# Four reorderings and one unsplit weight matrix in a two-layer decoder trunk

## The chip, the core and the metric

The kernel runs on one core of one Trainium2 chip. The metric is the device time of one launch in microseconds (us). The time before is 1378.09 us, the median of 3 runs (1377.64 to 1379.01).

## What is computed

The reference takes `x` (1 x 256 x 1024, float32) through two layers. Cut to what matters here, a layer is:

```python
u = x @ w_in[i]                                  # 1024 -> 512 pool + 512 value + 512 gate
y_pool = pool_mixer(u_pool, pool_w[i], pool_scale[i])
v = u_val * sigmoid(u_gate)                      # causal depthwise convolution, 31 taps, on v
y_conv = silu(layer_norm(conv(v) + b_dw)) @ conv_pw[i]
x = layer_norm(ALPHA * x + concat(y_pool, y_conv) @ w_out[i])
f = swiglu(x, w1, w3, w2)              if i == 0          # dense, 2816 wide
f = sum over the top 2 of 8 experts of gate * swiglu(x)   # i == 1, 3584 wide each
x = layer_norm(ALPHA * x + f)
x = x + sigmoid(x @ ple_gate_w[i]) * (p[i] @ ple_w[i])    # the embedding's gate
```

All weights are float32; those of the eight experts alone are 352 MB.

## The kernel before

**Tiles.** The 256 tokens are two halves `h` of 128 rows. Activations lie row by row in `xr[h]` (128 x 1024) and, for the matmuls, transposed in `xT[h]`. A float32 product is made as three matmuls of a cheaper type, float32r: each operand is split into a rounded part H and a rest L, and H·H, H·L and L·H are summed (`mm`, L339 to L349). `to_xT` (L335) transposes four 128 x 128 blocks on TensorE (L332), rounds them on ScalarE (L317) and takes the rest on VectorE (L318).

**Weights.** The class `Weights` (L75) holds one list of all weight items in the order of their use. `advance` (L122) loads each piece of 1 MB through SyncE's queue (L114), rounds it on ScalarE (L143, the "cast") and takes the rest on VectorE (L158, "the rests"). Loads, rounded items and temporaries share a pool of 19 slots; `hl` limits the slots of live rounded items, `temps` is set aside for temporaries, and `cap` says up to which item a `get` may go ahead of what it needs. `prepare(name, n)` makes items now, `n` of them or all. Names in `DIRECT` (L38) are not split: they are used as loaded, with the unrounded activations `x.f`, in one float32 matmul each (L341).

**Order.** Every engine runs its instructions in the order in which the program names them; nothing is scheduled behind its back. So where a `prepare` stands decides what its casts and rests delay. Six places matter here.

1. The start. L298 and L299 make the matrix `shift` (used first by the narrow experts' `fold`, L1044) from `con`, a block of constants; L299 is ScalarE's first instruction. Then come warm-up matmuls, `table(AF.Sigmoid)`, and at L1197 to L1199 the splits of the two halves of `x` and the first weights (`wg00`, `wv00`).
2. `mixer` (L462) begins with `diagonals(0)` (L494, L497): 16 ScalarE instructions that make the diagonal matrices of eight convolution taps; `conv(0)` (L503) uses them. In the second layer `value(0, 0, late)` carries in its middle the transposes of the second half of `xr` (`late`), and `gate(0, 1)` is the first that needs them.
3. `moe` (L838): the first expert's first matrix `w1e0_0` is multiplied with both halves, and between the matmuls of the second half the router's (L859, L861) and the sort of its results (`route`, L940; `positions`, L973) are placed:

```python
        W.prepare("w3e0_0", None)
        table(AF.Sigmoid)
        ...
        proj(ids, p1[0], xT[0])
        to_xT(xT[1], xr[1], 0)
        router(0, range(KD))
        to_xT(xT[1], xr[1], 1)
```

4. `experts` (L1037): 55 blocks of one expert's 512 hidden columns each, with first matrix `w1`, third `w3`, and the block before's `w2`. In the last block `cap` stands below the second item of the previous `w2` until that is needed (L1062, L1094).
5. The end of `moe`, L919 to L938: `last(h)` adds the last expert to `yacc[h]`, the norm of each half follows (`norm_begin`, then `norm_apply` for two column blocks, L413 and L414), `emit` makes the embedding, and `prepare` makes the gate's weights between them.
6. `embed_gate` (L1138) for the last layer: for column block c = 0 both halves, then for c = 1 both halves, the very last in two pieces of 256 columns (L1157). The second half's transposes are `late(0)` and `late(1)`, in the first of the four products.

Of the kernel before, what the change touches and what calls it, by code (L numbers as in the profile page):

```python
# [17 lines left out]
P = 128  # L18
# [3 lines left out]
KD = D // P  # L22
# [12 lines left out]
ND = len(DENSE_CHUNKS)  # L35
SLOTS = 19
HL_START, HL_PRE, HL_FIRST, HL_SECOND, HL_MOE = 8, 12, 8, 6, 10
DIRECT = ("pw0", "pw1", "wo00", "wo01")  # L38
DT = 23
MORE_AT = 53  # L40
WARM = 16
# [4 lines left out]
WU_EARLY = 2  # L46
# [5 lines left out]
EM = 3, 0  # L52
GL = 6
END = ((0, 256), (256, 256))
# [139 lines left out]
def trunk(ctx: ExitStack, tc: tile.TileContext, a: dict, out: bass.AP):  # L194
    nc = tc.nc
# [9 lines left out]
    def acc(name, k=None):  # L205

        if k is None:
            k = at[0] % 4
            at[0] += 1
        return pacc.tile([P, 512], F32, tag=f"acc{k}", name=name)  # L210
# [85 lines left out]
    H = P // 2  # L296
    shift = cp.tile([P, P], F32R, name="shift")
    nc.gpsimd.memset(shift[:, H:].bitcast(F32), 0.0)  # L298
    nc.scalar.copy(shift[:, :H], ident[:, H:])  # L299
    wr = tl("m2", [KD, NE])  # L300
    nc.gpsimd.dma_start(wr, a["router"])
    neghalf = cp.tile([P, 1], F32, name="neghalf")
# [19 lines left out]
    def new_xT(f=None):  # L322
        return [Split(tl(f"xH{h}", [KD, P], F32R), tl(f"xL{h}", [KD, P], F32R), None if f is None else f[:, h])
                for h in range(2)]
# [10 lines left out]
    def to_xT(dst, src, c):  # L335

        split_into(dst[:, 4 * c:4 * c + 4, :], transposes(src[:, c * 512:(c + 1) * 512], 4))
# [124 lines left out]
    def mixer(l, xT, xr, late, loads):  # L462
# [31 lines left out]
        def diagonals(b):  # L494
            for i in range(2):
                for k in range(TAPS - DT):
                    nc.scalar.activation(dg[:, i * 8 + k], ident, AF.Copy, scale=weight(2 * b + i, DT + k))  # L497
# [8 lines left out]
        def gate(b, h, between=None):  # L506
            pg = acc("ps_g")
            proj(W.names[f"wg{b}{l}"], pg, xT[h], free=h == 1, also=lambda k: k == GB and between and between())
            nc.scalar.activation(vb[b][h], pg[:, :256], AF.Sigmoid)

        def value(b, h, between=None):
            pv = acc("ps_v")
            proj(W.names[f"wv{b}{l}"], pv, xT[h], free=h == 1, also=lambda k: k == GB and between and between())
            nc.vector.tensor_mul(vb[b][h], pv[:, :256], vb[b][h])
# [3 lines left out]
            copy(vT[b][:, :, 32 + h * P:32 + (h + 1) * P], transposes(vb[b][h], 2))  # L518

        W.temps = TEMPS_MIX  # L520
        diagonals(0)

        gate(0, 0)
        if l == 0:
            gate(0, 1)
            value(0, 0)
        else:
            value(0, 0, late)
            gate(0, 1)
        W.prepare(f"wg1{l}")  # L530
        value(0, 1, lambda: turn(0, 0))
# [306 lines left out]
    def moe(l, xr, gb1, mix, project):  # L838
# [6 lines left out]
        sc = norm_begin(xr[1], mix[1], lambda: to_xT(xT[0], xr[0], 1))  # L845
        for c in range(2):
            norm_apply(gb1, xr[1], sc, c)
        W.prepare("w3e0_0", None)
        table(AF.Sigmoid)

        p1 = [acc("p1") for _ in range(2)]
# [13 lines left out]
        to_xT(xT[1], xr[1], 0)  # L865
        router(0, range(KD))
        to_xT(xT[1], xr[1], 1)
        W.hl = HL_SECOND
        routed = []

# [45 lines left out]
        last = experts(ranks, gates, xr, yacc, (selT, gsl, xg), lambda: hidden(g, 512, 0),  # L916
                       lambda: over(ci, beyond, gate, xr, yacc), end)
        gb, (ple, emit, _) = late["gains"], late["ple"]
        xT2 = new_xT()  # L919
        table(AF.Sigmoid)  # L920
        last(0)
        sc = [norm_begin(yacc[0], None)]
        W.prepare(f"gate0{l}", 2)
        emit(EM[0])
        for c in range(2):
            norm_apply(gb, yacc[0], sc[0], c)
        to_xT(xT2[0], yacc[0], 0)
        emit(EM[1])
        last(1)
        W.prepare(f"gate0{l}", 3)  # L930
        to_xT(xT2[0], yacc[0], 1)
        emit(4 - EM[0] - EM[1])
        sc.append(norm_begin(yacc[1], None))
        W.prepare(f"gate0{l}", 4)
        for c in range(2):
            norm_apply(gb, yacc[1], sc[1], c)
        W.prepare(f"gate1{l}", None)
        return xT2, yacc, lambda c: to_xT(xT2[1], yacc[1], c), ple  # L938

    def route(lg):  # L940
# [96 lines left out]
    def experts(ranks, gates, xr, yacc, nxt, first, more, end):  # L1037
# [9 lines left out]
        for i, (e, c) in enumerate(BLOCKS):  # L1047
# [11 lines left out]
            p1 = mmt("p1")  # L1059
            final = i == len(BLOCKS) - 1  # L1060
            if final:
                W.cap = W.names[f"w2e{prev[0]}_{prev[1]}"][1]  # L1062
            both(f"w1e{e}_{c}", [p1], [xg])
            if made is not None:
                prev[3] = made()
# [23 lines left out]
            if final:  # L1089
                down(ids[:1], paccs, pgT, pc == 0, False, True)  # L1090
                if narrow:
                    fold(p3, lo[:, 1])
                    g = glu(s_, p3, 512, par, gsl)
                W.cap = W.names[f"w2e{e}_{c}"][-1] + 1  # L1094
                W.hl = HL_PRE
                down(ids[1:], paccs, pgT, False, pc == FE - 1, True, 2)
            else:
                down(ids, paccs, pgT, pc == 0, pc == FE - 1, True)
                if narrow:
                    fold(p3, lo[:, 1])  # L1100
                    g = glu(s_, p3, 512, par, gsl)
# [36 lines left out]
    def embed_gate(l, xT, late, xr, ple, last):  # L1138

        xTn = None if last else new_xT()  # L1140

        def combine(h, c, ps, i=0, n=512):

            sg = tl(f"s{h}", [512])[:, i:i + n]
            cs = slice(c * 512 + i, c * 512 + i + n)
            nc.scalar.activation(sg, ps[:, :n], AF.Sigmoid)  # L1146
            nc.vector.tensor_mul(sg, sg, ple[:, h, cs])  # L1147
            nc.vector.tensor_add(xr[h][:, cs], sg, xr[h][:, cs])  # L1148
            if last:
                nc.sync.dma_start(out[h * P:(h + 1) * P, cs], xr[h][:, cs])  # L1150

        for c in range(2):
            ids = W.names[f"gate{c}{l}"]
            for h in range(2):
                if last and c and h:

                    for i, n in END:  # L1157
                        ps = acc("ps_gate")
                        for k in range(KD):
                            mm(ps[:, :n], xT[h][:, k, :], W.get(ids[k // 2]), (ALL, k % 2, slice(i, i + n)),  # L1160
                               k == 0, k == KD - 1)
                        combine(h, c, ps, i, n)
                    continue
                ps = acc("ps_gate")
                proj(ids[:2], ps, xT[h], last=False, free=h == 1)
                if c == h == 0 and not last:
                    late()
                    W.prepare(f"gate1{l}")
                if c and h == 0 and not last:
                    to_xT(xTn[0], xr[0], 0)  # L1170

                def between(k):
                    if c == h == 0 and last and k == GL:
                        late(0)
                    if c and h and k == GK:
                        to_xT(xTn[0], xr[0], 1)
                proj(ids[2:], ps, xT[h], 4, first=False, free=h == 1, also=between)
                if c == h == 0 and last:
                    late(1)
                combine(h, c, ps)  # L1180
                if c and h == 0 and not last:
                    W.prepare(f"wg1{l + 1}")
            if c == 0 and not last:
                W.prepare(f"wv0{l + 1}")
        if not last:
            W.temps = TEMPS_MIX
            W.hl = HL_PRE
            W.prepare(f"wv1{l + 1}", None)
            W.prepare(f"wu{l + 1}", WU_EARLY)
        return xTn, lambda: [to_xT(xTn[1], xr[1], c) for c in range(2)]  # L1190

    warm = tl("cat", [512], mybir.dt.bfloat16)
# [4 lines left out]
    for h in range(2):  # L1197
        split_into(xT[h], xF[:, h])
        W.prepare("wg00" if h == 0 else "wv00")  # L1199
    late = lambda: None  # L1200
    loads = mixer_loads(0)
    for l in range(L):
# [100 lines left out]
```

## Time and profile before

| | us |
|---|---|
| median of 3 runs | 1378.09 |
| the profiled execution, its own time | 1376.18 |
| its span, first to last instruction | 1374.4 |
| TensorE (PE) matmuls busy | 1317.2 (96%) |
| VectorE (DVE) busy | 1173.5 (85%) |
| ScalarE (ACT) busy | 921.8 (67%) |
| mean granted TensorE clock | 0.986 of full |

The page of the profile gives busy times and shares of the span, groups of instructions by line, and waits; the timeline gives each instruction's start and duration in us and, in square brackets, how long its engine sat idle before it and what ended that. Runs of like instructions are merged ("x16"). PEld is TensorE's weight load, SPq and POOLq the queues of SyncE and GpSimd that issue transfers. A matmul's duration holds its way through the pipeline: what a row of matmuls costs is read from the distance of their starts. The granted clock has two levels, 1.2 GHz (0.50) and 2.4 GHz (1.00).

### The profile page before, as it was taken

The numbers are of one execution on the slowest core, as the hardware profiler recorded it, in microseconds if no ns is written. First come the engines' busy times: TensorE is split into PE (matmuls) and PEld (weight loads), VectorE is DVE, ScalarE is ACT, GpSimd is POOL, SyncE is SP. The second block draws the span as 40 slices with busy tenths as digits, with TensorE's granted clock in tenths as the row PEclk, the third lists the DMA queues.
The fourth block names the chain that finished last, engine by engine and source line by source line (L and its number), as shares of the span: only waits on it lengthen the run. The fifth ranks groups of instructions, "written<-read, shape, count | busy, mean of one in ns | idle before, by whom it ended". The sixth has DMA issues, their size and how long they took to land. (4 is left out here: it accounts for less than half of the span.)

```text
span 1374.4 us, 17077 instructions
## 1 busy us (share of the span) xinstructions
PE 1317.2 (96%) x6314; PEld 1084.8 (79%) x6314; DVE 1173.5 (85%) x1102; ACT 921.8 (67%) x863; POOL 26.0 (2%) x33
## 2 busy tenths in 40 slices
PE   6999999999999999999999999999999999999777
PEld 5868888888967788878888878888887888888556
DVE  3987755466786989999999999999999999999885
ACT  5534544336333768887887887888787888898662
POOL 0000000010000200000000000000000000000000
PEclk8999999999998999999999999999999999999999
DMA  9436555526554499999999999999999999999850
GB/s 375 157 139 217 214 191 195 191 91 242 210 218 157 180 341 405 420 418 359 422 420 394 410 421 379 397 421 405 396 420 404 379 419 414 388 377 420 353 213 31
DMA packets 62172, 433.09 MB, mean 315 GB/s; under 512 B 6960, under 2 KB 7472, under 8 KB 11008
## 3 DMA queue, kind: packets, MB, share of 16 engines
q1 hardware_dynamic: 60336, 425.60, 78.5%
q0 software_dynamic: 1168, 4.23, 0.9%
q10 hardware_dynamic: 576, 2.10, 0.4%
q8 instruction: 51, 0.84, 0.2%
q14 instruction: 41, 0.34, 0.1%
HBM read 430.85 MB, written 1.05 MB: 314 GB/s over the span
## 5 line engine op out<-in xcount | busy, mean ns | idle before, releaser
L158 DVE TENSOR_TENSOR w<-w 128x2048 fp32r<-128x2048 f32 (+1 forms) x460 | 891.8, 1987 | 56.4 <-ACT w L143 49.8
L143 ACT CAST w<-w 128x2048 fp32r<-128x2048 f32 (+1 forms) x460 | 750.8, 1672 | 134.7 <-PE p L348 42.7
L344 PE MATMUL p<-w,xH 128*128 128x512 f32 (+1 forms) x1096 | 433.5, 396 | 9.5 <-ACT w L143 6.6
L349 PE MATMUL p<-w,xL 128*128 128x512 f32 (+1 forms) x648 | 250.9, 387 | 1.3 <-DVE xL L318 1.3
L348 PE MATMUL p<-w,xH 128*128 128x512 f32 (+1 forms) x648 | 250.2, 386 | 0.4 <-DVE w L158 0.4
L344 PEld LDWEIGHTS p<-w,xH 128*128 128x128 f32 x1096 | 207.6, 189 | 51.8 <-ACT w L143 7.0
L344 PE MATMUL y<-w,gH 128*128 128x512 f32 x448 | 176.2, 393 | 3.1 <-DVE gH L379 2.4
L346 PE MATMUL p<-w,xH 128*128 128x512 f32 x448 | 175.8, 392 | 0.0
L349 PEld LDWEIGHTS p<-w,xL 128*128 128x128 f32 x648 | 122.4, 189 | 26.7 <-DVE xL L318 1.8
L348 PEld LDWEIGHTS p<-w,xH 128*128 128x128 f32 x648 | 122.6, 189 | 24.6 <-DVE w L158 1.3
L344 PEld LDWEIGHTS y<-w,gH 128*128 128x128 f32 x448 | 84.6, 189 | 21.6 <-DVE gH L379 3.1
L346 PEld LDWEIGHTS p<-w,xH 128*128 128x128 f32 x448 | 85.0, 190 | 16.9
L346 PE MATMUL y<-w,gH 128*128 128x512 f32 x224 | 88.3, 394 | 1.9 <-DVE w L158 1.9
L349 PE MATMUL y<-w,gL 128*128 128x512 f32 x224 | 87.4, 390 | 1.2 <-DVE gL L318 1.2
L348 PE MATMUL y<-w,gH 128*128 128x512 f32 x224 | 87.3, 390 | 0.0
L484 DVE SCALAR_TENSOR_TENSOR yc<-w,vec,yc 128x256 f32<-128x256 f32 x176 | 70.4, 478 | 0.0
L645 ACT ACTIVATE s<-p 128x512 f32<-128x512 f32 (+1 forms) x69 | 41.2, 599 | 27.7 <-PE p L349 27.7
L318 DVE TENSOR_TENSOR gL<-tr,gH 128x512 fp32r<-128x512 f32 x38 | 25.7, 684 | 32.7 <-ACT gH L317 32.7
L346 PEld LDWEIGHTS y<-w,gH 128*128 128x128 f32 x224 | 42.6, 190 | 11.0 <-DVE w L158 2.3
L317 ACT CAST gH<-tr 128x512 fp32r<-128x512 f32 x38 | 21.9, 587 | 43.6 <-PE tr L332 43.0
L349 PEld LDWEIGHTS y<-w,gL 128*128 128x128 f32 x224 | 42.0, 188 | 10.4 <-DVE gL L318 1.6
L348 PEld LDWEIGHTS y<-w,gH 128*128 128x128 f32 x224 | 42.1, 188 | 9.0
(223 smaller groups left out, 1415.9 us busy)
## 6 DMA issues: line engine op xcount, KB each, us to landing
w<-in_exp_w SPq DMA_DIRECT2D x336, 1024.0 KB, 8.7
w<-in_dense_w SPq DMA_DIRECT2D x33, 1024.0 KB, 5.0
w<-in_w_out SPq DMA_DIRECT2D x8, 1024.0 KB, 6.4
w<-in_ple_gate_w SPq DMA_DIRECT2D x8, 1024.0 KB, 5.1
w<-in_w_gv SPq DMA_DIRECT2D x6, 1024.0 KB, 7.2
w<-in_w_u SPq DMA_DIRECT2D x4, 1024.0 KB, 10.2
w<-in_w_gv SPq DMA_DIRECT2D x4, 512.0 KB, 7.3
w<-in_w_small SPq DMA_DIRECT2D x2, 1024.0 KB, 9.1
```

The lines of the kernel that those rows point to most:

```text
L143: nc.scalar.copy(h, w)
L158: engine.tensor_tensor(l, w, h.bitcast(F32), op=ALU.subtract)
L317: nc.scalar.copy(dst.h, src)
L318: nc.vector.tensor_sub(dst.l, src, dst.h.bitcast(F32))
L344: nc.tensor.matmul(ps, x.h, wh, start=start, stop=False)
L346: nc.tensor.matmul(ps, x.h, wl, start=False, stop=stop)
L348: nc.tensor.matmul(ps, x.h, wl, start=False, stop=False)
L349: nc.tensor.matmul(ps, x.l, wh, start=False, stop=stop)
L484: nc.vector.scalar_tensor_tensor(yc[:, ct], src, weight(ct, t), yc[:, ct], op0=ALU.mult, op1=ALU.add)
L645: nc.scalar.activation(s_[:, :nf], p1[:, :nf], AF.Silu)
```

## The change

It makes `shift` after the splits of `x` and the first weights; moves the second layer's `diagonals(0)` behind `value(0, 0, late)`; moves `prepare("w3e0_0")` behind the second half's transposes; puts the last layer's second gate matrix (`gate11`) into `DIRECT`, for which `xT2` gets unrounded copies `f` in a new temporary; raises `cap` earlier in the last block; and reorders the end: column block 0 of the first half is normed and transposed ahead of column block 1, and the gate runs both column blocks of the first half ahead of the second half, with the second half's transposes in the second product.

```diff
-DIRECT = ("pw0", "pw1", "wo00", "wo01")
+DIRECT = ("pw0", "pw1", "wo00", "wo01", "gate11")
...
     nc.gpsimd.memset(shift[:, H:].bitcast(F32), 0.0)
-    nc.scalar.copy(shift[:, :H], ident[:, H:])
...
         W.temps = TEMPS_MIX
-        diagonals(0)
+        if l == 0:
+            diagonals(0)
...
             value(0, 0, late)
+            diagonals(0)
             gate(0, 1)
...
-        W.prepare("w3e0_0", None)
         table(AF.Sigmoid)
...
         to_xT(xT[1], xr[1], 1)
+        W.prepare("w3e0_0", None)
         W.hl = HL_SECOND
...
-        xT2 = new_xT()
+        xT2 = new_xT(W.temp([2, KD, P]))
         table(AF.Sigmoid)
         last(0)
         sc = [norm_begin(yacc[0], None)]
+        W.prepare(f"gate0{l}", 1)
+        emit(EM[0])
+        norm_apply(gb, yacc[0], sc[0], 0)
+        to_xT(xT2[0], yacc[0], 0)
+        norm_apply(gb, yacc[0], sc[0], 1)
         W.prepare(f"gate0{l}", 2)
-        emit(EM[0])
-        for c in range(2):
-            norm_apply(gb, yacc[0], sc[0], c)
-        to_xT(xT2[0], yacc[0], 0)
+        to_xT(xT2[0], yacc[0], 1)
         emit(EM[1])
         last(1)
         W.prepare(f"gate0{l}", 3)
-        to_xT(xT2[0], yacc[0], 1)
         emit(4 - EM[0] - EM[1])
...
-        W.prepare(f"gate1{l}", None)
+        W.prepare(f"gate1{l}")
...
             if final:
-                W.cap = W.names[f"w2e{prev[0]}_{prev[1]}"][1]
+                W.cap = W.names[f"w2e{e}_{c}"][-1] + 1
...
-                W.cap = W.names[f"w2e{e}_{c}"][-1] + 1
                 W.hl = HL_PRE
...
+        def pieces(h, c):
+            for i, n in END:
+                ps = acc("ps_gate")
+                for k in range(KD):
+                    it = W.get(ids[k * len(ids) // KD])
+                    mm(ps[:, :n], xT[h][:, k, :], it, (ALL, k % it["k"], slice(i, i + n)), k == 0, k == KD - 1)
+                combine(h, c, ps, i, n)
+        if last:
+            for h in range(2):
+                for c in range(2):
+                    ids = W.names[f"gate{c}{l}"]
+                    if c and h:
+                        pieces(h, c)
+                        continue
+                    ps = acc("ps_gate")
+                    n = len(ids) // 2
+                    proj(ids[:n], ps, xT[h], last=False)
+                    proj(ids[n:], ps, xT[h], 4, first=False, also=lambda k: k == GL and c and late(0))
+                    if c:
+                        late(1)
+                    combine(h, c, ps)
+            return None, None
...
         split_into(xT[h], xF[:, h])
         W.prepare("wg00" if h == 0 else "wv00")
+    nc.scalar.copy(shift[:, :H], ident[:, H:])
```

The rest of the diff takes the last layer's branches out of the old loop of `embed_gate`.

## Rows read from the trace of the kernel before

**Rows 1.** Busy time by engine, 460 to 1270 us, summed: the experts' blocks.
```profile
sum 810.00, PE 799.12 PEld 658.55 DVE 787.91 ACT 670.61 POOL 3.43; mean PE 99.89 PEld 82.32 DVE 98.49 ACT 83.83 POOL 0.43
```

**Rows 2.** Line L143 (casts), 460 to 1270 us: longest of what it waited for.
```profile
  PE p L348: 42.7, 41
```

**Rows 3.** Timeline of ACT, 0 to 40 us: start, duration, instruction [idle before].
```profile
12.63 0.24 ACT L299 CAST shift<-con 128x64 fp32r<-128x64 f32 x1 [10.62 <-DMA con<-in_con]
...
19.97 4.79 ACT L497 ACTIVATE w<-con,vec 128x128 f32<-128x128 f32 x16
...
34.89 3.87 ACT L143 CAST w<-w 128x1024 fp32r<-128x1024 f32 x4
```

**Rows 4.** Timeline of PE, 0 to 40 us: the first matmul after the warm-up.
```profile
16.32 0.58 PE L344 MATMUL ps_g<-w,xH 128*128 128x256 f32 x1 [9.67 <-ACT w L143]
```

**Rows 5.** Transfer issued at 3.14 us (second half of wv00): size, us to landing.
```profile
w<-in_w_gv SPq DMA_DIRECT2D x1, 512.0 KB, 8.9
```

**Rows 6.** Transfer issued at 9.46 us (second half of wu0): size, us to landing.
```profile
w<-in_w_u SPq DMA_DIRECT2D x1, 1024.0 KB, 13.5
```

**Rows 7.** Timeline of ACT, 318 to 372 us: the second mixer's diagonals.
```profile
330.73 4.79 ACT L497 ACTIVATE w<-con,vec 128x128 f32<-128x128 f32 x16
```

**Rows 8.** Timeline of PE, same stretch: first and last of gate(0, 1)'s 24 matmuls.
```profile
336.31 0.58 PE L344 MATMUL ps_g<-w,xH 128*128 128x256 f32 x1 [3.28 <-ACT xH L317]
...
340.69 0.28 PE L349 MATMUL ps_g<-w,xL 128*128 128x256 f32 x1
```

**Rows 9.** Windows: us, busy PE PEld DVE ACT POOL, PEclk, DMA, GB/s: that product.
```profile
336.10:339.30 3.20, 2.99 (x12) 2.77 (x13) 1.62 (x3) 0.63 (x2) 0.00 (x0) 0.50 0.29 123
```

**Rows 10.** Timeline of DVE, 396 to 466 us: w3's rests, router's result, mask.
```profile
427.32 4.62 DVE L158 TENSOR_TENSOR w<-w 128x1024 fp32r<-128x1024 f32 x4
...
437.92 0.17 DVE L876 COPY lg<-ps_r 128x8 f32<-128x8 f32 x1 [4.51 <-PE ps_r L861]
...
440.23 0.17 DVE L966 TENSOR_SCALAR msk<-rank 128x16 f32<-128x16 f32 x1
```

**Rows 11.** Timeline of PE, 396 to 466 us: second half's first product; the selection.
```profile
430.52 0.50 PE L344 MATMUL p<-w,xH 128*128 128x512 f32 x1 [1.48 <-ACT xH L317]
...
444.97 0.38 PE L767 MATMUL ps_sel<-con,m 128*128 128x128 f32 x2
```

**Rows 12.** Timeline of DVE, 1270 to 1335 us: a whole item's rest; last block's product.
```profile
1309.62 2.28 DVE L158 TENSOR_TENSOR w<-w 128x2048 fp32r<-128x2048 f32 x1
...
1316.48 0.75 DVE L654 SCALAR_TENSOR_TENSOR g<-p,gsl,s 128x512 f32<-128x512 f32 x1 [4.24 <-PE p L1045]
```

**Rows 13.** Timeline of PE, 1270 to 1335 us: the last block's second matrices.
```profile
1319.48 0.80 PE L346 MATMUL y<-w,gH 128*128 128x512 f32 x1 [1.94 <-DVE w L158]
...
1324.22 0.50 PE L344 MATMUL y<-w,gH 128*128 128x512 f32 x1 [1.06 <-DVE gH L379]
```

**Rows 14.** The page, groups of instructions: rounding of four transposed blocks on ACT.
```profile
L317 ACT CAST gH<-tr 128x512 fp32r<-128x512 f32 x38 | 21.9, 587 | 43.6 <-PE tr L332 43.0
```

**Rows 15.** Timeline of PE, 1318 to 1376 us: transposes and the four gate products.
```profile
1336.40 0.66 PE L332 MATMUL tr<-con,w 128*128 128x128 f32 x4 [2.10 <-DVE w L414]
...
1339.80 0.39 PE L344 MATMUL ps_gate<-w,xH 128*128 128x512 f32 x1
...
1352.26 0.51 PE L349 MATMUL ps_gate<-w,xL 128*128 128x512 f32 x1 [4.02 <-DVE xL L318]
...
1358.99 0.39 PE L344 MATMUL ps_gate<-w,xH 128*128 128x512 f32 x1
...
1364.20 0.39 PE L349 MATMUL ps_gate<-w,xL 128*128 128x512 f32 x1
...
1370.06 0.28 PE L349 MATMUL ps_gate<-w,xL 128*128 128x256 f32 x1
```

**Rows 16.** Timeline of PE: unsplit float32 matmuls, 256 and 512 columns (two records each).
```profile
346.99 7.08 PE L503 MATMUL ps_c<-w 128*128 128x256 f32 x32
...
394.76 5.31 PE L341 MATMUL ps_o<-w,cat 128*128 128x512 f32 x12
```

More of the change, by code (lines that the diff above doesn't have):

```diff
@@ L1154, in embed_gate @@
             for h in range(2):
[L1155 to L1163, printed above, removed]
                 ps = acc("ps_gate")
                 proj(ids[:2], ps, xT[h], last=False, free=h == 1)
-                if c == h == 0 and not last:
+                if c == h == 0:
                     late()
                     W.prepare(f"gate1{l}")
-                if c and h == 0 and not last:
+                if c and h == 0:
                     to_xT(xTn[0], xr[0], 0)
                 def between(k):
-                    if c == h == 0 and last and k == GL:
-                        late(0)
                     if c and h and k == GK:
@@ L1177, in embed_gate @@
                 proj(ids[2:], ps, xT[h], 4, first=False, free=h == 1, also=between)
-                if c == h == 0 and last:
-                    late(1)
                 combine(h, c, ps)
-                if c and h == 0 and not last:
+                if c and h == 0:
                     W.prepare(f"wg1{l + 1}")
-            if c == 0 and not last:
+            if c == 0:
                 W.prepare(f"wv0{l + 1}")
[L1185 to L1189, printed above, removed]
+        W.temps = TEMPS_MIX
+        W.hl = HL_PRE
+        W.prepare(f"wv1{l + 1}", None)
+        W.prepare(f"wu{l + 1}", WU_EARLY)
         return xTn, lambda: [to_xT(xTn[1], xr[1], c) for c in range(2)]
```

## The prediction

> **What bounds the kernel now.** I read the windows over the experts' blocks first. In those 810 us PE is busy 799 and DVE 788 [rows 1], and the list of what the casts there waited for names PE and DVE alone, with 42.7 us for PE first [rows 2], and no transfer: PE is the bound of the body, and the transfers follow it by the slots that it frees. The body has no clock of its own, so whatever starts it earlier ends it earlier by as much. Then I read the timelines of the three places where the order is changed ahead of the body, and of the end. The reader is to see the same thing at each: PE idle because ACT or DVE is doing something in program order that nobody needs yet. At the start ACT's first instruction waits 10.62 us for a block of constants [rows 3], and PE stands behind it for 9.67 [rows 4]. In the second mixer PE idles 3.28 behind 16 diagonals [rows 7, 8]. In the experts' layer PE waits for a split that is queued behind w3's casts and rests [rows 10, 11]. At the end it waits 1.94 for a rest [rows 13], and later 4.02 [rows 15].
>
> The profiled execution took 1376.18 us; the sum is made against that, and the median of the runs lies 1.9 above it.
>
> **The start.** `shift` is used only by the experts, so moving its copy (0.24) costs nothing. What goes is the wait in front of `x`. ACT now takes `x`, wg00 and wv00 as they land. The last of these was issued at 3.14 and takes 8.9 [rows 5]: 12.0. Its cast is a quarter of 3.87 [rows 3], then the copy follows, whose constants are in by 12.63: the diagonals start at 13.25 instead of 19.97, a gain of 6.7. This is one end. But PE gains more, since it no longer begins with all four products queued up: a rest is a quarter of 4.62 [rows 10], so wv00 is whole at 14.2, and by then both `gate` products are nearly done. A product of 24 matmuls of 256 columns costs 2.9 (48 from 1364.20 to 1370.06, 0.122 each [rows 15]). value(0, 0) runs from about 14.7 to 17.6, value(0, 1) to 21.0 with its transposes. ACT is through the diagonals at 18.0, through two sigmoids and wg10's two casts at 20.7; DVE has its rests at 22. gate(1, 0) ends at 24.5, and wu's four casts start at 25.1 instead of 34.89 [rows 3]: 9.8. wu lands at 9.46 + 13.5 = 23.0 [rows 6]; that is the other end, a gain of 11.9. I take **-9.7**, since every step of it is in rows. Behind wu the taps are DVE's own chain and move as a whole. SP's and POOL's issues keep their order; the loads that wait for slots come earlier with PE.
>
> **The second mixer.** The 16 diagonals (4.79 [rows 7]) stand in front of the sigmoid and the rounding of the second half, on which gate(0, 1) waits. Moved behind the rounding they run from about 332.4 to 337.2, beside gate(0, 1) and value(0, 1), and `conv(0)` needs them only after gate(1, 0). Queued behind them is gate(0, 1)'s sigmoid, which is wanted at the end of value(0, 1), about 338.7. So the 3.28 of idle goes. With it goes a slow start: the 24 matmuls from 336.31 to 340.69 [rows 8] take 4.50 with the last, 1.6 more than 2.9, because the granted clock stands at 0.50, the lower level of 1.2 GHz, after the idle stretch [rows 9]. Together **-4.9**; the ends are -3.3 (idle alone) and -5.1.
>
> **The first expert.** w3e0_0's four casts and rests move behind the second half's split. PE can then begin the second half's product 1.48 earlier, at 429.05 [rows 11], and doesn't stop again for the L part. But the rests now stand in front of the router's result on DVE. The second half's last split is rounded at 429.6; four casts take 3.9 and end at 433.5, four rests end at about 435.3. Before, the second half's result was read at 437.92 and the mask was ready at 440.40 [rows 10], 2.5 later. Now both halves are read after the rests: mask at 435.3 + 0.35 + 2.5 = 438.2. PE meanwhile is done with six of the eight steps at 435.0 and meets `positions`, which needs the mask: **a new wait of 3.1 us**, with two steps of the product and the selection queued behind it. Those take 1.0 and 1.4, so the selection comes at 440.6 instead of 444.97 [rows 11]: -4.4. Against that stands the clock: an idle stretch of 3.1 is nearest to the 3.28 of [rows 8], which cost 1.6; I take 1.2 of it, because part of the work behind is DVE's. **-3.2**; ends 0 (product slow throughout) and -5.5 (rests in gaps, no wait).
>
> Here a rule can be weighed. The trace has an idle stretch of 2.10 ahead of the first transposes at the end [rows 15] and one of 3.28 with a slow start [rows 8]. The Trainium skill, "TensorE: Matmul & The Clock Gate", section "HAM oscillation — how this bites in real kernels", says that a wait for data puts the clock back to its lower level, so that each group after such a wait starts cold and pays again. By the rule both idle stretches that this change makes (here and at the end) pay; without it the sum below would be 2.4 lower.
>
> **The last block.** With `cap` raised, the previous w2's second item is cast right behind its first, and the last block's two w2 items during its w3. On ACT these fill idle time; the copy of `p3` comes 1 us later, which DVE hides. On DVE the queue grows: the first item's rest ends at 1311.9 [rows 12], and three more rests of 2.24 (the next starts 2.2 after the last) and the hidden part's short subtraction (some 0.4) now stand ahead of the block's product, which starts at 1319.0 instead of 1316.48 [rows 12]. But PE no longer stops 1.94 for the second item's rest [rows 13]: it is through these matmuls at about 1318.5, waits 1.2 for the product, and starts the last `down` at 1321.3 instead of 1324.22 [rows 13]. **-2.8**; ends 0 and -3.3.
>
> **The end.** Removed: gate11's four casts and four rests (4.6 on DVE), behind which PE waited 4.02 [rows 15]. Added: four copies for `f` on ACT, each about a rounding's 0.59 [rows 14], all behind the rounding that PE needs, so hidden but for ACT's queue; and dearer matmuls. An unsplit matmul is two records: 12 take 5.15 until the next instruction, 0.86 each pair at 512 columns; 32 take 7.08, 0.44 at 256 [rows 16]. Split, 24 of 512 columns take 5.4 (1358.99 to 1364.20 [rows 15]) and 48 of 256 take 5.9. So the two products with gate11 cost 8 x 0.86 + 16 x 0.44 = 14.0 instead of 11.3: +2.7 on PE. By the Trainium skill, "FP8 and Floating Point Precision", section "TensorE Precision Notes", true float32 takes four passes; four for three would make it +3.8.
>
> The new order has its own price. One rest fewer stands ahead of the first norm block, which ends 0.6 earlier (the transposes that follow it at 1336.40 [rows 15]), but the second block waits on DVE until the first is transposed, rounded and split (0.66 and 0.59 by [rows 14, 15], the split on DVE taken as 0.65): it ends at 1339.15, and behind it are queued its transposes, last(1) and the last of the embedding, 3.1 of PE. The gate starts at 1342.2 instead of 1339.80 [rows 15]. From there PE runs without a stop: 5.4 + 6.9 + 0.9 of transposes + 5.4 + 7.1 = 25.7, and the second half's norm, done at about 1349, is needed at 1353. It ends at 1367.9 instead of 1370.2: -2.2, and +1.2 for the clock after the 2.7 of idle ahead of the gate: **-1.0**; ends +2.9 (all that the matmuls cost, nothing back) and -2.8. The `f` tile takes one of 19 slots; the gate's loads are issued long before they are needed.
>
> **The sum:** -9.7 - 4.9 - 3.2 - 2.8 - 1.0 = -21.6: 1354.6 for a profiled execution, **1356.5** for the median. A measurement of this kernel can tell about 0.2% (2.8 us) from no change.
>
> **Rivals.**
> - *The start is held by the transfers and ACT alone*: -6.7 in place of -9.7, 1359.5. For it: ACT still runs everything in one queue, and PE may be granted the lower clock while its first products are sparse. Against it: ACT's diagonals end before PE needs them.
> - *The clock stays up* at both new idle stretches: 1354.1. For it the 2.10 of [rows 15]; against it [rows 8].
> - *The router pays it all back*: the rests ahead of it and the slow clock eat what the split gains, 0 for the first expert: 1359.7.
> - *The end is a loss*: the float32 matmuls cost 2.7 and the reordered norms only shift the wait: +2.9, 1360.4.
> - *The experts' stream runs dry* (slower): w3e0_0's rests free four load slots about 3.4 later, the next loads come later, and from then on every block's casts wait for a transfer. Breaks even at 21.6 / 55 blocks = 0.39 us a block; at 0.5 it is 1384. Against it: no cast waited for a transfer in 810 us [rows 2].
> - *A part does nothing*: the cap, say, because a slot and not the cap held the cast: 1359.3.
>
> **Chances.** The forecast 0.55, transfers at the start 0.12, clock up 0.10, router 0.08, end 0.06, cap 0.05, stream 0.04. All but the last are faster by far more than 0.2%: faster 0.93; slower 0.03; same 0.04 for the stream near its point of balance or several losses together. Range: all the good ends together give 1349.5; two bad ends together (start and first expert, or start and end) give about 1363. I take 1350 to 1363.5.
>
> **What would show it.** Right: `x` rounded from about 4.3 us, wu's casts at 25; no idle in front of gate(0, 1) in the second mixer; PE waiting some 3 us at L977's matmuls for the mask; the last block's product later on DVE than the end of `p3`'s copy; 456 casts and 456 rests instead of 460, 72 split matmuls gone and 48 records of unsplit ones come; the gate without a stop. Wrong: casts that wait for a transfer in the body; the body longer than before; the gate's first matmul later than 3 us after its old place, counted from the last `down`.

## The result and the profile after

The changed kernel takes **1355.93 us** (median of 4 runs, 1354.12 to 1356.65) against 1378.20 for the kernel before (4 runs): a ratio of 0.9836, 95% interval 0.9819 to 0.9853. The forecast was 1356.5, in a range of 1350 to 1363.5. The profiled execution took 1355.96, its span 1354.2 against 1374.4.

I compare the two traces at places that both have, each as its start before and after:

| place | before | after | difference | added by this stretch |
|---|---|---|---|---|
| first mixer's `conv(0)` (PE) | 34.41 | 23.51 | -10.90 | -10.9, the start |
| second mixer's first `pw` matmul (PE) | 401.24 | 386.24 | -15.00 | -4.1, the second mixer |
| first expert's `ps_s` (PE, L893) | 449.20 | 433.05 | -16.15 | -1.15, the first expert |
| 25th of L808's `ps_sc` matmuls of the experts (PE) | 1282.31 | 1266.14 | -16.17 | 0, the body |
| last block's `ps_sc` (PE, L808) | 1328.38 | 1309.55 | -18.83 | -2.7, the last block |
| end of the span | 1374.42 | 1354.19 | -20.23 | -1.4, the end |

The table has the lines after the change. They are shifted by one or two: `mm`'s L344, L348 and L349 are L343, L347 and L348 now, L892 is L893, L807 is L808.

**The page after**, totals and the two largest groups:

```profile
PE 1313.5 (97%) x6290; PEld 1079.0 (80%) x6290; DVE 1170.0 (86%) x1098; ACT 919.6 (68%) x862; POOL 25.9 (2%) x33
...
L158 DVE TENSOR_TENSOR w<-w 128x2048 fp32r<-128x2048 f32 (+1 forms) x456 | 887.3, 1992 | 58.6 <-ACT w L143 52.0
L143 ACT CAST w<-w 128x2048 fp32r<-128x2048 f32 (+1 forms) x456 | 747.1, 1677 | 132.8 <-PE p L347 42.7
```

456 casts and rests, as the prediction counted. The casts still wait first for PE, 42.7 us, the number of [rows 2]: the body did not change.

**The start**, timeline of ACT after (start, duration, instruction, idle before in brackets), to set beside [rows 3]:

```profile
4.86 1.05 ACT L316 CAST xH<-w 128x1024 fp32r<-128x1024 f32 x1 [2.63 <-DMA w<-in_xT]
...
12.76 4.79 ACT L496 ACTIVATE w<-con,vec 128x128 f32<-128x128 f32 x16
...
23.71 0.38 ACT L508 ACTIVATE s<-ps_g 128x256 f32<-128x256 f32 x1 [1.06 <-PE ps_g L348]
23.99 3.87 ACT L143 CAST w<-w 128x1024 fp32r<-128x1024 f32 x4
```

`x` is rounded as it lands, the diagonals start at 12.76, and the last sigmoid, which waits for PE's gate(1, 0), releases wu's casts at 23.99.

**The second mixer**: timelines of ACT, DVE and PE after, to set beside [rows 7, 8]:

```profile
320.30 1.08 ACT L316 CAST xH<-tr 128x512 fp32r<-128x512 f32 x2
321.26 4.79 ACT L496 ACTIVATE w<-con,vec 128x128 f32<-128x128 f32 x16
...
317.53 4.62 DVE L158 TENSOR_TENSOR w<-w 128x1024 fp32r<-128x1024 f32 x4
322.07 1.28 DVE L317 TENSOR_TENSOR xL<-tr,xH 128x512 fp32r<-128x512 f32 x2
...
322.81 0.39 PE L348 MATMUL ps_g<-w,xL 128*128 128x256 f32 x1 [0.44 <-DVE xL L317]
```

The wait of 3.28 is gone. One of 0.44 has come: the second half's rests `xL` now stand behind four rests of weights on DVE.

**The first expert**: timelines of DVE and PE after, to set beside [rows 10, 11], and two windows (us, busy PE PEld DVE ACT POOL with instructions, PEclk, DMA share, GB/s). The last view has two places on PE before:

```profile
415.64 4.63 DVE L158 TENSOR_TENSOR w<-w 128x1024 fp32r<-128x1024 f32 x4 [0.25 <-ACT w L143]
420.19 0.16 DVE L877 COPY lg<-ps_r 128x8 f32<-128x8 f32 x1
...
422.76 0.17 DVE L968 TENSOR_SCALAR msk<-rank 128x16 f32<-128x16 f32 x1
...
423.08 0.57 PE L979 MATMUL ps_pos<-msk,con 128*128 128x8 f32 x2 [3.09 <-DVE msk L968]
...
427.92 0.63 PE L768 MATMUL ps_sel<-con,m 128*128 128x128 f32 x2
...
433.05 1.88 PE L893 MATMUL ps_s<-s,m 128*128 128x512 f32 x4
```

```profile
423.00:429.70 6.70, 6.62 (x25) 5.96 (x26) 2.04 (x15) 1.39 (x4) 0.00 (x0) 0.50 0.51 188
430.00:433.00 3.00, 3.00 (x29) 3.00 (x29) 0.69 (x1) 0.58 (x1) 0.00 (x0) 1.00 0.71 292
```

```profile
442.46 0.28 PE L977 MATMUL ps_pos<-msk,con 128*128 128x8 f32 x2
...
449.20 1.88 PE L892 MATMUL ps_s<-s,m 128*128 128x512 f32 x4
```

The forecast new wait is there to the decimal: w3's rests, then the router's result, then the mask, and PE idle for 3.09. Behind it the granted clock is 0.50, its lower level of 1.2 GHz, for 6.7 us. The selection's matmuls take 0.63 where [rows 11] had 0.38.

Ahead of the positions it is the other way round. Two windows within the second half's first six steps and the router's matmuls, before and after:

```profile
431.70:441.70 10.00, 9.10 (x29) 7.87 (x30) 4.84 (x24) 2.18 (x4) 0.00 (x0) 0.50 0.77 295
```

```profile
413.80:419.80 6.00, 6.00 (x37) 5.06 (x35) 4.85 (x5) 4.38 (x5) 0.00 (x0) 1.00 0.41 130
```

Before, this work took 11.9 us (430.52 to 442.46), 1.34 of it a wait, and 10.2 of it at 0.50 (431.6 to 441.8); after, it takes 6.0 at 1.00 (413.80 to 419.83).

**The last block and the end**: timeline of PE after, to set beside [rows 13, 15]:

```profile
1305.39 0.50 PE L343 MATMUL y<-w,gH 128*128 128x512 f32 x1 [0.92 <-DVE gH L378]
...
1316.43 0.66 PE L331 MATMUL tr<-con,w 128*128 128x128 f32 x4 [0.97 <-DVE w L413]
...
1320.03 0.63 PE L331 MATMUL tr<-con,w 128*128 128x128 f32 x4 [2.94 <-ACT w L143]
...
1324.37 0.39 PE L343 MATMUL ps_gate<-w,xH 128*128 128x512 f32 x1
...
1329.84 6.17 PE L340 MATMUL ps_gate<-w 128*128 128x512 f32 x14
1336.28 1.02 PE L340 MATMUL ps_gate<-w 128*128 128x512 f32 x2
...
1343.04 7.07 PE L340 MATMUL ps_gate<-w 128*128 128x256 f32 x32
```

The 1.94 in front of the last `down` is gone, the wait in front of the gate is now 0.97 + 2.94, and from 1324.37 on PE runs without a stop: the 4.02 of [rows 15] is gone too.

### The profile page after: what moved, and what is told of

Read it like the earlier page. It is cut to its first block, busy times and chain, and to the rows that moved or that the text cites. A ratio compares the mean times of both kernels' runs of the same rounds, so it can differ in the third digit from the quotient of the medians.

```text
span 1354.2 us, 17024 instructions
## 1 busy us (share of the span) xinstructions
PE 1313.5 (97%) x6290; PEld 1079.0 (80%) x6290; DVE 1170.0 (86%) x1098; ACT 919.6 (68%) x862; POOL 25.9 (2%) x33
## 5 line engine op out<-in xcount | busy, mean ns | idle before, releaser
L143 ACT CAST w<-w 128x2048 fp32r<-128x2048 f32 (+1 forms) x456 | 747.1, 1677 | 132.8 <-PE p L347 42.7
L343 PE MATMUL p<-w,xH 128*128 128x512 f32 (+1 forms) x1096 | 433.2, 395 | 8.2 <-DVEq L1034 6.8
L347 PE MATMUL p<-w,xH 128*128 128x512 f32 (+1 forms) x648 | 249.7, 385 | 0.4 <-DVE w L158 0.4
L348 PE MATMUL p<-w,xL 128*128 128x512 f32 (+1 forms) x648 | 250.0, 386 | 0.0
L343 PEld LDWEIGHTS p<-w,xH 128*128 128x128 f32 x1096 | 207.1, 189 | 50.3 <-ACT w L143 7.2
L343 PE MATMUL y<-w,gH 128*128 128x512 f32 x448 | 175.4, 392 | 2.5 <-DVE gH L378 2.5
L348 PEld LDWEIGHTS p<-w,xL 128*128 128x128 f32 x648 | 122.0, 188 | 24.8
L347 PEld LDWEIGHTS p<-w,xH 128*128 128x128 f32 x648 | 122.3, 189 | 24.5 <-DVE w L158 1.2
L343 PEld LDWEIGHTS y<-w,gH 128*128 128x128 f32 x448 | 84.1, 188 | 20.9 <-DVE gH L378 3.6
L348 PE MATMUL y<-w,gL 128*128 128x512 f32 x224 | 87.4, 390 | 1.2 <-DVE gL L317 1.2
L347 PE MATMUL y<-w,gH 128*128 128x512 f32 x224 | 87.3, 390 | 0.0
L348 PEld LDWEIGHTS y<-w,gL 128*128 128x128 f32 x224 | 42.0, 188 | 10.4 <-DVE gL L317 1.6
L347 PEld LDWEIGHTS y<-w,gH 128*128 128x128 f32 x224 | 42.1, 188 | 9.0
```

The source lines that it names most:

```text
L143: nc.scalar.copy(h, w)
L343: nc.tensor.matmul(ps, x.h, wh, start=start, stop=False)
L347: nc.tensor.matmul(ps, x.h, wl, start=False, stop=False)
L348: nc.tensor.matmul(ps, x.l, wh, start=False, stop=stop)
```

## The experiments

Differences are against the changed kernel's profiled execution. Kernels with the same code up to a place reach it up to 0.9 us apart (the first mixer's `conv(0)` at 22.99 to 23.84), so I compare the length of a stretch between two places of one run. Two of these are steady: the body, from the experts' first `ps_sc` matmul to the 25th, takes 646.63 to 646.77 in all fourteen profiles, before and after included; and from the last block's `ps_sc` to the end it takes 44.63 to 44.67 in eight of the nine profiles with the changed end (45.46 in the ninth). The nine runs of the changed kernel lie between 1351.74 and 1356.65, so the time of one run decides nothing below some 5 us. Diffs are against the changed kernel. The kernel before took 1378.90, 1378.49 and a median of 1377.67 on the three chips used.

**The four parts, each put back by itself.** First the copy of `shift`:

```diff
     nc.gpsimd.memset(shift[:, H:].bitcast(F32), 0.0)
+    nc.scalar.copy(shift[:, :H], ident[:, H:])
...
         W.prepare("wg00" if h == 0 else "wv00")
-    nc.scalar.copy(shift[:, :H], ident[:, H:])
```

> The changed kernel with shift's copy back in front of the splits of x; all else as changed. Theory (the parts are separate and the body behind them is rigid): wu's first casts come 10.9 us later than in the changed kernel (34.9 instead of 23.99), every later landmark is late by the same 10.9, and the profiled time is 1366.9. Rival (the parts share a gain: what the start gives is partly given back at a later wait, so that undoing it costs less): under 1364.

1362.61, that is +6.7. PE timeline, and the window ahead of it:

```profile
433.84 0.36 PE L980 MATMUL ps_pos<-msk,con 128*128 128x8 f32 x2
...
440.66 1.88 PE L894 MATMUL ps_s<-s,m 128*128 128x512 f32 x4
```

```profile
425.90:432.60 6.70, 6.70 (x23) 5.73 (x23) 6.31 (x16) 3.81 (x6) 0.00 (x0) 0.50 0.44 157
```

The second mixer's `conv(0)` is 11.0 later and `ps_pos` 10.8, so the start is worth what the traces gave it. But here the low clock falls ahead of the mask, in time that PE would have waited; `ps_pos` follows without a wait, and `ps_s` 6.8 later instead of 10.0. The mask, ready at 433.69, comes just before PE does. The router's wait, not the start, gave back some 3 us; the other 1.1 goes in the last block's stretch, 42.3 here and 43.4 after the change (see the `cap` below).

Then the diagonals, for both layers at the head of `mixer`:

```diff
-        if l == 0:
-            diagonals(0)
+        diagonals(0)
...
             value(0, 0, late)
-            diagonals(0)
             gate(0, 1)
```

> The changed kernel with the second mixer's diagonals back in front of its first product. Theory: PE idles 3.3 us ahead of gate(0, 1) with a slow start behind it; landmarks are the same up to there and 4.1 to 4.4 late from the second conv's matmuls on; profiled time about 1360.2. Rival (the diagonals' gain is part of the first expert's, because the wait only moves): under 1358.

1358.99. From the first mixer's `conv(0)` to the second's it takes 5.5 more than after the change; by the end 3.0 are left. Of the difference, 0.4 is this run's earlier start, 1.6 is lost at `ps_s`, where the low clock behind the wait is shorter (429.6 to 433.0), and 0.5 in the last block's stretch.

w3's `prepare` back in front:

```diff
         for c in range(2):
             norm_apply(gb1, xr[1], sc, c)
+        W.prepare("w3e0_0", None)
         table(AF.Sigmoid)
...
         to_xT(xT[1], xr[1], 1)
-        W.prepare("w3e0_0", None)
```

> The changed kernel with w3e0_0's casts and rests back in front of the second half's split. Between the two traces this part was worth 1.15 us at ps_s (L893), against 3.2 forecast. Theory: the new 3.1 us wait for the mask and the low clock behind it eat most of it; undone, the time is 1.0 to 1.5 longer, about 1357.1, and the two waits of 1.5 and 1.3 are back in place of the one of 3.1. Rival (the part is worth the 3.2 of the forecast, and another part lost the rest): 1359.

1356.87. PE timeline:

```profile
427.90 0.28 PE L979 MATMUL ps_pos<-msk,con 128*128 128x8 f32 x2
...
434.64 1.88 PE L893 MATMUL ps_s<-s,m 128*128 128x512 f32 x4
```

`ps_pos` is 4.8 later, `ps_s` only 1.6 (1.3 without the 0.3 by which this run was late from the start on). So the move wins 4.5 at the positions and loses 3.2 behind them. As in the kernel before, the low clock now stands ahead of the positions (417.2 to 427.4).

And the last block's `cap`:

```diff
-                W.cap = W.names[f"w2e{e}_{c}"][-1] + 1
+                W.cap = W.names[f"w2e{prev[0]}_{prev[1]}"][1]
...
                     g = glu(s_, p3, 512, par, gsl)
+                W.cap = W.names[f"w2e{e}_{c}"][-1] + 1
                 W.hl = HL_PRE
```

> The changed kernel with the cap of the last block as it was. Theory: the wait of 1.9 us for the second item's rest is back; the last down starts 3.1 late against the block before; time about 1359.0. Rival (a slot, not the cap, held the cast): no change, 1356.0.

1358.69. Its PE timeline has the wait of [rows 13] again:

```profile
1303.32 0.79 PE L345 MATMUL y<-w,gH 128*128 128x512 f32 x1 [1.94 <-DVE w L158]
```

From the 25th `ps_sc` to the last block's it takes 46.3, as before the change (46.1); the changed kernel takes 43.4, and the kernels that keep this part 42.3 to 43.8. The part is worth 2.9 between this pair.

The same stretch holds a longer wait of PE that no edit here touches, by the timeline after the change:

```profile
1274.93 0.77 PE L343 MATMUL p<-w,xH 128*128 128x512 f32 x1 [6.76 <-DVEq L1034]
```

The profile puts it down to the branch in `over` (L1034), and in the kernel before and with the `cap` put back to a cast behind that. PE waits 5.94 to 6.88 there in all fourteen profiles, 6.56 in the kernel before, which is a part of the spread of this stretch.

**Is it the clock, or the wait?** Twelve matmuls of 512 columns, whose result is not used, fill PE's wait for the mask:

```diff
             if k == KP:
                 gate, msk = routed
+                keep_warm(12)
                 routed.extend(positions(msk, gate, xr))
```

> The changed kernel with 12 dummy matmuls (512 columns, their result is not used) on PE in the new wait for the mask. Theory (the forecast's size for the first expert failed by the clock: in the changed kernel the granted clock is 0.50 from 423.0 to 429.8, right behind the wait, and the matmuls from ps_pos to ps_s take 9.97 us instead of 6.74 before): PE stays at 1.00, ps_s comes at about 430.0 instead of 433.05, time about 1353. Rival (what stands behind the wait is DVE's chain, not the clock): ps_s within 0.5 of 433.05, time 1356 or, with the dummies in the way, more.

1351.40. PE timeline and window:

```profile
422.77 0.36 PE L980 MATMUL ps_pos<-msk,con 128*128 128x8 f32 x2 [0.49 <-DVE msk L969]
...
429.58 1.88 PE L894 MATMUL ps_s<-s,m 128*128 128x512 f32 x4
```

```profile
423.00:429.70 6.70, 6.70 (x55) 6.39 (x55) 2.42 (x14) 1.66 (x4) 0.00 (x0) 1.00 0.80 307
```

The mask comes at the same time, but `ps_s` follows in 6.8 instead of 10.0: 3.2 is the price of the clock alone.

**Is the wait itself needed?** The casts stay where they are, the rests go behind the selection:

```diff
-        W.prepare("w3e0_0", None)
+        W.prepare("w3e0_0", None, "later")
...
         sel, cc = select(0, posm, gate, 0, 0)
+        W.rests(nc.vector)
```

> The changed kernel with w3e0_0's rests (not its casts) put behind the selection on DVE, so that the router's result is read when PE has it. Theory (the rests in front of the router's result make the wait of 3.1 us, and the wait makes the low clock): mask at about 419.7, no wait in front of ps_pos, no low clock, ps_s at 426.5 to 428 instead of 433.05, time 1349.5 to 1351. Rival (the wait only moves, to the gathered rows' split behind the rests): ps_s at 430 to 433, time 1353 to 1356.

1348.79. `ps_pos` at 419.31, with no idle time of PE from 405 to 422:

```profile
419.31 0.33 PE L980 MATMUL ps_pos<-msk,con 128*128 128x8 f32 x2
...
426.10 1.88 PE L894 MATMUL ps_s<-s,m 128*128 128x512 f32 x4
```

7.0 earlier at `ps_s`, 7.3 at the end; against the changed kernel's second profile (below), with its shorter low clock, it is 5.3 at `ps_s`. The same two edits with the old start:

```diff
     nc.gpsimd.memset(shift[:, H:].bitcast(F32), 0.0)
+    nc.scalar.copy(shift[:, :H], ident[:, H:])
...
-        W.prepare("w3e0_0", None)
+        W.prepare("w3e0_0", None, "later")
...
+        W.rests(nc.vector)
...
         W.prepare("wg00" if h == 0 else "wv00")
-    nc.scalar.copy(shift[:, :H], ident[:, H:])
```

> The kernel with w3e0_0's rests behind the selection, and shift's copy back in front of the splits of x. In the changed kernel, undoing the start cost 11.0 us up to ps_pos and only 6.6 at the end, because the low clock fell into the wait for the mask and not behind it. Theory (it is that wait, with the clock, which swallows part of what comes earlier): without the wait the start is worth its whole 11 us, so this run is 10.5 to 11.5 longer than the one without this undoing. Rival (the body or the end swallows it): 6 to 8 longer.

1361.12, 12.3 more than without the old start: 10.75 at `ps_s`, and 1.6 near the end, where its clock is low twice (from 1308.8 and from 1322.5). The total is outside both forecasts. Up to the body the start is worth its whole 11 us when no wait stands between, which is what the first experiment left open; the 1.6 lies in the last block's stretch and the end (43.8 and 45.5 instead of 43.0 and 44.6).

**The end.** gate11 split again, and no unrounded activations:

```diff
-DIRECT = ("pw0", "pw1", "wo00", "wo01", "gate11")
+DIRECT = ("pw0", "pw1", "wo00", "wo01")
...
-        xT2 = new_xT(W.temp([2, KD, P]))
+        xT2 = new_xT()
```

> The changed kernel with gate11 split as before (three float32r matmuls; four more casts and rests, no copies f), the new order kept. The forecast: unsplit matmuls cost 2.7 us more on PE, and what they give is that the four rests are gone from DVE. Theory (in the new order the rests would have stood in front of nothing that PE needs soon, since the second half's split comes 6 us later, so that the unsplit matrix alone is a loss): time 2 to 2.8 us shorter, 1353.2 to 1354. Rival (the rests are still in the way): the same or longer, 1356 and more.

1354.44. From the last block's `ps_sc` to the end it takes 43.70 instead of 44.64, in spite of a wait for a rest within the gate, by its PE timeline:

```profile
1330.82 0.50 PE L347 MATMUL ps_gate<-w,xH 128*128 128x512 f32 x1 [1.16 <-DVE w L158]
```

From its first matmul the gate takes 29.0 instead of 29.8, so without the wait of 1.16 the split form is 2.0 shorter. The time meets neither forecast: the rests are in the way once. The two products themselves differ by more, by the starts in the changed kernel and in this run: 16 unsplit records of 512 columns take 6.87 and 24 split matmuls 5.47, 32 records of 256 columns 6.90 and 48 split ones 5.75. That is 2.6, and the prediction had 2.7; some 0.6 more went in the product that holds the wait. In the new order the unsplit matrix is a loss of 0.9.

**The changed kernel once more**, on the chip of the following three, five runs:

> The changed kernel once more, on the chip and in the call of the three below, as what they are compared with. All theories: 1355 to 1357.

1354.06 (1351.74 to 1355.47), ratio 0.9823, interval 0.9810 to 0.9837. The mask comes as before, but the low clock begins later and is over sooner; PE timeline and window:

```profile
423.01 0.36 PE L979 MATMUL ps_pos<-msk,con 128*128 128x8 f32 x2 [3.10 <-DVE msk L968]
...
431.44 1.88 PE L893 MATMUL ps_s<-s,m 128*128 128x512 f32 x4
```

```profile
425.00:428.40 3.40, 3.40 (x15) 3.00 (x14) 0.53 (x4) 0.86 (x2) 0.00 (x0) 0.50 0.47 133
```

8.4 from `ps_pos` to `ps_s`: one kernel, the same wait, and 1.5 less to pay. The wait of 3.1 stands in seven profiles. In four the low clock lasts 6.8 us and this stretch 9.87 to 10.03, in three 3.4 us and 8.41 to 8.43.

The old order of the four products:

```diff
-            for h in range(2):
-                for c in range(2):
+            for c in range(2):
+                for h in range(2):
...
-                    proj(ids[n:], ps, xT[h], 4, first=False, also=lambda k: k == GL and c and late(0))
-                    if c:
+                    proj(ids[n:], ps, xT[h], 4, first=False, also=lambda k: k == GL and not c and not h and late(0))
+                    if not c and not h:
                         late(1)
```

> The changed kernel with the four gate products in the old order (both halves for column block 0, then both for 1; the second half's transposes in the first product). Theory (what the new order gives is that the second half's norm is no longer awaited): late(0) comes at 1328.5, before the norm is done at 1330.5, so PE waits some 2 us for the transposes and another 0.5 to 1 for the split, and the time is 2 to 4 longer than the changed kernel's. Rival (without gate11's rests the old order would do as well): within 0.7.

1354.79. From the last block's `ps_sc` to the end it takes 45.13 instead of 44.64: 0.5 longer, not 2 or more, so the rival was right. With gate11 unsplit, nothing in the old order waits for its rests.

Both norms of the first half ahead of its transposes:

```diff
         norm_apply(gb, yacc[0], sc[0], 0)
-        to_xT(xT2[0], yacc[0], 0)
         norm_apply(gb, yacc[0], sc[0], 1)
+        to_xT(xT2[0], yacc[0], 0)
```

> The changed kernel with both norm blocks of the first half ahead of its first transposes on DVE. In the changed kernel PE idles 0.97 and 2.94 there and then has the low clock from 1320.7 to 1324.1, up to the gate's first matmul at 1324.37. Theory (DVE, waiting for the first block's transposes and rounding, holds the second norm block): the second transposes come about 2 earlier, the low clock goes, the gate starts 2.5 to 4 earlier, time 1352 to 1353.5. Rival (the weights' rests or last(1) hold the gate anyway): gate within 1 of 1324.4, time 1355 to 1356.

1354.64, which is within the spread of the changed kernel, so the time decides nothing. PE timeline:

```profile
1317.72 1.05 PE L331 MATMUL tr<-con,w 128*128 128x128 f32 x4 [0.88 <-DVE w L413]
...
1327.24 0.50 PE L347 MATMUL ps_gate<-w,xH 128*128 128x512 f32 x1 [0.66 <-DVE w L158]
```

The wait of 2.94 shrank to 0.88, and a wait for a weight's rest came inside the gate. The gate's first matmul comes at 1322.09, 2.3 earlier, which is between the two forecasts. Last `ps_sc` to end: 43.58, 1.1 shorter.

**All three gains together**: rests later, norms first, gate11 split (the diffs above), five runs:

```diff
-DIRECT = ("pw0", "pw1", "wo00", "wo01", "gate11")
+DIRECT = ("pw0", "pw1", "wo00", "wo01")
...
-        W.prepare("w3e0_0", None)
+        W.prepare("w3e0_0", None, "later")
...
+        W.rests(nc.vector)
...
-        xT2 = new_xT(W.temp([2, KD, P]))
+        xT2 = new_xT()
...
-        to_xT(xT2[0], yacc[0], 0)
         norm_apply(gb, yacc[0], sc[0], 1)
+        to_xT(xT2[0], yacc[0], 0)
```

> The changed kernel with three things more: w3e0_0's rests behind the selection (-7.0 alone), both norm blocks of the first half ahead of its transposes, and gate11 split again (-1.5 alone). Theory (they lie in separate stretches and add up): 1356 - 7 - 2.5 - 1.5 = 1345, ratio to the kernel before 0.976. Rival (the clock at the end gives part of it back, as it did between other runs): 1347 to 1349.

**1347.52** (1347.04 to 1350.88), ratio to the kernel before 0.9781, interval 0.9767 to 0.9794; 6.5 less than the changed kernel on the same chip. The profile is of its longest execution; a window, and the PE timeline at the end:

```profile
415.10:421.90 6.80, 6.80 (x23) 5.83 (x23) 3.40 (x21) 5.52 (x8) 0.00 (x0) 0.50 0.46 154
```

```profile
1325.54 0.50 PE L347 MATMUL ps_gate<-w,xH 128*128 128x512 f32 x1 [2.45 <-DVE w L158]
```

The sum of 1345 was not reached; the rival's range was. The end gives little: 43.79 from the last `ps_sc`, no better than either edit alone. With the gate begun earlier and four rests more, PE waits 2.45 for DVE.

## Why the prediction came out right, and where its steps did not

**The start, -9.7: measured -10.9.** The steps held: PE's gate(1, 0), not the transfer of wu, releases wu's casts. The last 1.2 came in small parts along that chain: by PE's timeline gate(1, 0) began at 20.42 where the prediction had 21.0, and ended at 23.7 where it had 24.5; the casts followed 0.3 behind, where it had 0.6. With the earlier start the granted clock is 1.00 from 11.75 to 22 us, where the kernel before had 0.50. The prediction did not name one thing that goes with the copy: before, ScalarE's table was loaded twice at the start (0.73 and 12.89, 1.28 us each), since the copy stood ahead of `table(AF.Sigmoid)`; after, it is loaded once. The rival of -6.7 is out.

**The second mixer, -4.9: measured -4.1 at `pw`.** The diagonals are hidden and the slow start is gone. What the step left out is DVE's queue: four rests of weights in front of the split, and 0.44 of waiting; the other 0.4 stays open. Putting the diagonals back costs 5.5 rather than 4.1: in that run the clock is low for longer (323.8 to 330.6) than in the kernel before (336.0 to 339.4), and gate(0, 1) takes 5.6 instead of 4.5.

**The first expert, -3.2: measured -1.15. This is the step that failed**, by the words "an idle stretch of 3.1 is nearest to the 3.28 of [rows 8], which cost 1.6; I take 1.2 of it, because part of the work behind is DVE's". The mechanism was right to a decimal: a wait of 3.1 forecast, 3.09 measured, and `ps_pos` 4.4 earlier than the stretch ahead of it explains (-19.38 against -15.00), as forecast. The clock behind it was mis-sized: from `ps_pos` to `ps_s` takes 6.74 before, 9.97 after, 6.81 with the wait filled. That is 3.2, not 1.2; nothing on DVE covered any of it. How much is paid changes from one execution to the next. From `pw` to `ps_s` the move gains 1.1 to 1.3 in four of the seven profiles with this wait and 2.7 in the other three, where 1.6 was paid. The rival "the router pays it all back" is nearer in the four, the forecast in the three.

The step also holds a gain that it does not name. It lets the second half's six steps run in 5.95 us (429.05 to 435.0), as they then did (6.0); before, they took 11.9, and only 1.3 of the difference is waiting. The rest is the low clock, 431.6 to 441.8 in the kernel before, which the prediction did not read.

The Trainium skill, "TensorE: Matmul & The Clock Gate", section "HAM oscillation — how this bites in real kernels", says that work behind a wait for data starts cold. It says so of a kernel whose waits are mostly longer than these, so by that rule neither of the prediction's two idle stretches was sure to pay. This case agrees in part: behind the 3.1 of waiting PEclk falls to 0.50 within 0.6 us in four profiles and after 1.4 to 2.0 us in three, and filling the wait kept it at 1.00; but behind the 2.10 of [rows 15] it stayed at 1.00 up to 1353.2.

**The body, 0: measured 0.** 646.67 before, 646.69 after. The rival of a stream that runs dry is out.

**The last block, -2.8: measured -2.7**, and 2.9 with the cap put back. The product moves down DVE's queue and the wait of 1.94 goes, as argued.

**The end, -1.0: measured -1.4**, for partly wrong reasons. The gate's first matmul came 3.4 later against the last block (2.4 forecast), and PE then ran without a stop, 25.7 us to the end of its last matmul, as forecast. With 3.4, one of the prediction's own signs of being wrong came (a first matmul of the gate later than 3 us after its old place, counted from the last `down`: 18.98 behind it, 15.58 before), and the end gained all the same. The low clock from 1320.7 to 1324.1 lies ahead of the gate and is within the 3.4; the prediction had put its price, 1.2, behind. But the point "needed at 1353", for which both edits were held to be needed together, is immaterial: with the rest of the change in place, either one removes most of the 4.02 of [rows 15]. With the matrix unsplit the old order has no wait for rests; with the matrix split the new order waits 1.16. The second is the better, 43.70 against 45.13 from the last `ps_sc`, and both edits together lie between them at 44.64. The rival that the end is a loss is out, but half of it, the dearer matmuls, is real: 2.6 where the prediction had 2.7.

The Trainium skill, "FP8 and Floating Point Precision", section "TensorE Precision Notes", has four passes for true float32, which would be 3.8 by the prediction's working, an estimate; the runs show 2.6.

**Profile to median.** The prediction added 1.9 for the distance of the profile from the median. For the changed kernel that distance is nothing (1355.96 and 1355.93). The profiled executions differ by 20.2, not 21.6; the error of 1.4 in the sum and that of 1.9 here nearly cancel, and the miss of 0.6 is smaller than either. Within the sum the steps are off by -1.2, +0.8, +2.05, +0.1 and -0.4. Most of the mechanisms held; that the total came within 0.6, with one step off by 2, is luck. Three roundings in its working (14.0 for 13.9, -2.2 for -2.3, -2.8 for -2.9) change nothing.

## What to carry to other kernels

Ahead of a long stretch that is bound by one engine, every microsecond won at the head arrives at the end, but only if no wait stands between: a wait can swallow gains ahead of it, and here the clock behind it cost as much as the wait in four profiles of seven, and half as much in three. When a batch of work is moved out of one engine's way, read the queue that it lands in, here DVE's, and see what small result with a long chain behind it (the router's) now stands in line; moving only the rests once more was worth 5 to 7 us, a quarter to a third of the whole change. In this kernel a matrix left unsplit paid only where its rests were waited for.

## What was not expected of the hardware

The same wait of 3.1 us costs the 6.7 to 6.8 us of work behind it 1.6 or 3.2 more, by how long the clock stays low: 423.0 to 429.8 in one profile of the changed kernel, 425.0 to 428.4 in the other. The kernel is the same, so its order does not decide it. In the run with the old start the low clock fell ahead of `ps_pos`, and there was no wait.

The clock also falls with no idle time of PE close ahead: in the run with the old start PE shows no wait from 415 to 437, and is granted 0.50 from 425.9 to 432.6; in the last kernel it shows none from 405 to 423, and 0.50 from 415.1 to 421.9. In both the engine had been running the router's small matmuls (8 and 16 columns) when the clock fell. But the kernel with the rests moved runs the same instructions there and kept 1.00. Why the one and not the other is not settled. `ps_pos` comes at 423.00 in the last kernel's profile and at 419.31 with only the rests moved, which is about the 3 us by which that execution of the last kernel stands above its other four.
